# Sample-token attention in unsplit float32 on a tiled PE array

## The chip, the cores and the metric

The kernel runs on one core of a Trainium2 chip. The metric is the device time of one execution in microseconds (us). Three runs of the kernel before took 1849.01, 1849.45 and 1852.46 us; the median is 1849.45.

## The reference, cut to what matters

One decoder layer runs on a prompt of 1024 tokens and on 8 sequences of 4 new "sample" tokens each. The sample tokens attend to 1024 cached positions of their own sequence, which lie in pages of 128, and to the new tokens before them. This differential attention of the sample tokens is what the change touches: 4 heads, two score maps each (index m), and the second softmax is subtracted from the first with weight lambda.

```python
PAST_LEN, PAGE_SIZE, N_HEADS_A, HEAD_DIM_A = 1024, 128, 4, 64
...
def diff_attention(q, ks, vs, masks, lam):
    scale = HEAD_DIM_A ** -0.5
    s = jnp.concatenate([jnp.einsum('bqhmd,bkhmd->bhmqk', q, k, preferred_element_type=jnp.float32) * scale
                         for k in ks], -1)
    mask = jnp.concatenate(masks, -1)
    p = jax.nn.softmax(jnp.where(mask, s, -jnp.inf), axis=-1)
    a = (p[:, :, 0] - lam * p[:, :, 1]).astype(vs[0].dtype)
    offs = np.cumsum([0] + [k.shape[1] for k in ks]).tolist()
    return sum(jnp.einsum('bhqk,bkhe->bqhe', a[..., offs[i]:offs[i + 1]], vs[i]) for i in range(len(ks)))
```

The rest of the layer (projections, the HGRN2 branch, prompt attention, the gated merge, the convolutional FFN of width 2816) surrounds it and is unchanged.

## The kernel before, in words

The kernel writes each large float32 matrix product as three products of a high and a low half. `split` (lines 130 to 132) makes the halves: ScalarE (ACT) writes the high half in the format fp32r, VectorE (DVE) subtracts it from the source to get the low half. Such a product is then three TensorE (PE) matmuls, at lines 226 to 228 in `mm3` and 236 to 238 in `mm3s`. Small products are left in plain float32; the trace has two MATMUL records for each of those.

The order of the work: input projections, HGRN2, prompt attention, gates; then the merge of the first half of the prompt tokens; then `sample_attn`; then the FFN on the first half; then merge and FFN on the second half, with the sample tokens. The instructions of an engine are put in order when the program is built. `sample_attn` is written ahead of the FFN in the source, and the order that results has FFN matmuls (`mm<-hh,wh` and their like, 256 columns each) between those of the sample attention. At run time each engine goes through its list in that order; POOL's list also issues the gathers of cache pages.

`sample_attn` handles two groups (g) of four sequences (j). For the keys of a sequence it gathers two tiles of half the past (`pages`, line 715; 128 x 4 x 512 float32, 1 MB each; two buffers named `pg`). PE transposes each 128x128 piece (line 208, output `tp`, 32 a sequence), `split` turns PSUM into `kh` and `kl`, and two matmuls a head (lines 755 and 756, 64 columns of stationary queries, high beside low) give the scores in `ps_s`. ScalarE and VectorE fold them into `Pg`, whose 128 rows are 4 sequences x 32 (head, map, token). After the softmax, 8 small matmuls at line 792 turn `Pg` and subtract the second map, giving `aT`. For the values, VectorE and ScalarE split each gathered tile into `kh` and `kl`, and lines 816 and 817 multiply all four heads' rows by all four heads' values (512 columns); `hmask` keeps the diagonal blocks, and `select` (line 728) adds them up through a constant matrix. Line 801 does the same for the new tokens' values, and `sample_new_scores` (line 700), called before the last prompt head, made their scores.

Of the kernel before, what the change touches and what calls it, by code (L numbers as in the profile page):

```python
# [17 lines left out]
TP = 1024  # L18
TS = 32
# [12 lines left out]
C_SEL, C_SEL2, C_HM, C_M0, C_M1, C_CN, C_KEEP = 0, 128, 320, 324, 325, 326, 390  # L32
C_CAUS, C_ROPE, C_BD, C_IO, C_END = 390, 518, 1094, 1102, 1103
# [12 lines left out]
def hybrid_step(ctx: ExitStack, tc: tile.TileContext, I, O):  # L46
# [44 lines left out]
    sel2 = ck[:, C_SEL2:C_SEL2 + 192].rearrange("p (g c) -> p g c", c=32)  # L91
# [596 lines left out]

    def sample_new_scores():
        qbd_t = ring.get()  # L690
        qbd = qbd_t[:, :1024].rearrange("p (h b r) -> p h b r", b=8, h=4)
        V.memset(qbd_t[:, :1024], 0.0)
        for hh in range(4):
            for m in range(2):
                V.tensor_copy(qbd[m * 64:m * 64 + 64, hh, :, hh * 8 + m * 4:hh * 8 + m * 4 + 4],
                              qsm[m * 64:m * 64 + 64, hh].rearrange("p (b s) -> p b s", b=8))
# [5 lines left out]
        ring.put(qbd_t)  # L702

    def sample_attn(ap):
        def bank(tag):
            return ps_s.tile([128, 512], F32, tag="s", name="ps_s") if tag in ("sc", "av") else pst()

# [3 lines left out]
        def pages(nm, b, c):  # L711

            dst = ap.tile([128, 4, 512], F32, tag="pg", name="pg", bufs=2)
            i = b * 2 + c
            G.indirect_dma_start(dst.rearrange("p r e -> p (r e)"), None, crow[nm], bass.IndirectOffsetOnAxis(ap=idx[:, i:i + 1], axis=0))
            return dst

        def pair(tag):
            return ap.tile([128, 4, 256], F32R, tag=tag, name=tag, bufs=2)

        zero = ap.tile([128, 1], F32, name="zero")
        V.memset(zero, 0.0)
        osb = ap.tile([TS, 512], F32, name="osb")
        first = [True]

        def select(mk, sel):
            p = bank("ms")
            PE.matmul(p[:TS, :], lhsT=sel, rhs=mk, start=True, stop=True)
            if first[0]:
                evac("v", osb, p[:TS, :])  # L730
                first[0] = False
            else:
                V.tensor_tensor(osb, osb, p[:TS, :], ALU.add)

        def hmask(dst, src, np_):
            V.tensor_tensor(dst.rearrange("p (h e) -> p h e", h=4), src.rearrange("p (h e) -> p h e", h=4),
                            ck[:np_, C_HM:C_HM + 4][:, :, None].to_broadcast([np_, 4, 128]), ALU.mult)

        for g in range(2):
            qs = ap.tile([128, 4, 4, 2, 32], F32R, tag="qs", name="qs")  # L740
            V.tensor_copy(qs.rearrange("p b h x r -> p (b h x r)"), zero.to_broadcast([128, 1024]))
            for hh in range(4):
                for m in range(2):
                    r = slice(m * 64, m * 64 + 64)
                    c0 = hh * 8 + m * 4
                    src = qsm[r, hh, g * 16:g * 16 + 16].rearrange("p (b s) -> p b s", b=4)
# [4 lines left out]
            def scores(j, pr, ps, kth, ktl):  # L751
                for hh in range(4):
                    lq = qs[:, j, hh].rearrange("p x r -> p (x r)")
                    o = ps[:64, (pr % 2) * 256:(pr % 2 + 1) * 256]
                    PE.matmul(o, lhsT=lq, rhs=kth[:, hh], start=(hh == 0), stop=False)
                    PE.matmul(o, lhsT=lq, rhs=ktl[:, hh], start=False, stop=(hh == 3))
                if pr % 2:
                    pj = Pg[j * 32:j * 32 + 32, (pr // 2) * 512:(pr // 2) * 512 + 512]
                    evac("s", pj, ps[:32, :])
                    V.tensor_tensor(pj, pj, ps[32:64, :], ALU.add)  # L760

            late = None
            for j in range(4):
                b = g * 4 + j
                for pr in range(4):
                    if pr % 2 == 0:
                        ps = bank("sc")
                        kp = pages("cache_k", b, pr // 2)
                    kth, ktl = pair("kh"), pair("kl")
                    for c2 in range(2):  # L770
                        p = bank("kt").rearrange("p (h t) -> p h t", h=4)
                        for hh in range(4):
                            transpose(p[:, hh], kp[:, (pr % 2) * 2 + c2, hh * 128:(hh + 1) * 128])
                        split(p, kth[:, :, c2 * 128:c2 * 128 + 128], ktl[:, :, c2 * 128:c2 * 128 + 128])
                    if late:
                        scores(*late)
                    late = (j, pr, ps, kth, ktl)
            scores(*late)
# [6 lines left out]
            Cg = ap.tile([128, 128], F32, tag="Cg", name="Cg", bufs=2)  # L785
            V.tensor_scalar(Cg, selC, mx[:, 7:8], None, ALU.mult)
            aT = ap.tile([128, 8, 4, 2, 32], F32R, tag="aT", name="aT")
            for hf in range(2):
                p = bank("ms")
# [3 lines left out]
                pv = p.rearrange("p (c j r) -> p c j r", c=4, j=4)  # L793
                for c4 in range(4):
                    split(pv[:, c4], aT[:, hf * 4 + c4, :, 0], aT[:, hf * 4 + c4, :, 1])
            p = bank("ms")
# [3 lines left out]
            p = bank("ms")  # L800
            PE.matmul(p, lhsT=an, rhs=vs_, start=True, stop=True)
            mk = ap.tile([128, 512], F32, tag="mk", name="mk")
            hmask(mk, p, 128)
            select(mk, sel2[:, g])
            mk = None
            for j in range(4):
                b = g * 4 + j
                pav = bank("av")
                for c in range(8):
                    if c % 4 == 0:  # L810
                        vp = pages("cache_v", b, c // 4)
                    if c % 2 == 0:
                        vh, vl = (x.rearrange("p a b -> p (a b)").rearrange("p (r e) -> p r e", r=2) for x in (pair("kh"), pair("kl")))
                        split(vp[:, c % 4:c % 4 + 2], vh, vl)
                    la = aT[:, c, j].rearrange("p x r -> p (x r)")
                    PE.matmul(pav[:64], lhsT=la, rhs=vh[:, c % 2], start=(c == 0), stop=False)  # L816
                    PE.matmul(pav[:64], lhsT=la, rhs=vl[:, c % 2], start=False, stop=(c == 7))
                if j % 2 == 0:
                    mk = ap.tile([128, 512], F32, tag="mk", name="mk")
                r0 = (j % 2) * 64  # L820
                hmask(mk[r0:r0 + 64], pav[:64], 64)
                if j % 2:
                    select(mk, sel2[:, 2 + g * 2 + j // 2])
        ssq = ap.tile([TS, 4], F32, name="sssq")
        rs = ap.tile([TS, 4], F32, name="srs")
        sq = ap.tile([TS, 128], F32, name="ssq_")
        for hh in range(4):
            S.activation(sq, osb[:, hh * 128:(hh + 1) * 128], AF.Square, accum_out=ssq[:, hh:hh + 1])
        V.tensor_scalar(ssq, ssq, 1.0 / 128, EPS, ALU.mult, ALU.add)
        rstd(rs, ssq)  # L830
        p = bank("ms").rearrange("p (h t) -> p h t", h=4)
        for hh in range(4):
            V.tensor_scalar(osb[:, hh * 128:(hh + 1) * 128], osb[:, hh * 128:(hh + 1) * 128], rs[:, hh:hh + 1], None, ALU.mult)
            transpose(p[:, hh, :TS], osb[:, hh * 128:(hh + 1) * 128])
        oc = ap.tile([128, 4, TS], F32, name="soc")
        V.tensor_scalar(oc, p[:, :, :TS], SUBG, None, ALU.mult)
        G.dma_start(osc[4:8, :, TP:T].rearrange("h p t -> p h t"), oc)
# [350 lines left out]
def _consts():  # L1188
# [12 lines left out]
    j, q = r // 32, r % 32  # L1201
    h, m, s = q // 8, (q // 4) % 2, q % 4
# [82 lines left out]
```

## Time and profile before

| what | value |
|---|---|
| median of three runs | 1849.45 us |
| the profiled execution | 1850.71 us |
| its span, first to last instruction | 1848.5 us |
| PE busy | 1812.3 us, 98% of the span |
| DVE, ACT, POOL busy | 60%, 45%, 10% |
| mean granted TensorE clock | 0.994 of full speed |
| stretch with the sample attention | about 842 to 1151 us |

A busy PE in these views means that some matmul is under way. Matmuls overlap in the array, so a matmul's own duration (some 280 ns for 256 columns) is much longer than the time from its start to the next one's start (some 118 ns). What a matmul costs is read from starts, or from the chain of waits, which counts each stretch of time once.

### The profile page before, as it was taken

Reading aid. Unit: us, or ns where it says so; the run is one execution under the profiler, and the core shown is the slowest. Engines: PE = TensorE matmul, PEld = TensorE weight load, DVE = VectorE, ACT = ScalarE, POOL = GpSimd, SP = SyncE. Lnnn points to the kernel's source line nnn. Section 1 sums busy time; section 2 is a strip of 40 time slices with the busy share of each in tenths; the row PEclk is TensorE's granted clock in tenths of the full one; section 3 lists DMA queues with packets and bytes.
Section 4 is the critical chain, followed back from the end, with each engine's and each line's share of the span. In section 5 each row is a group of like instructions: output and inputs, shape, how many; then the busy total and the mean of one; then the engine's idle time right before and its main releaser. Section 6 shows DMA issues by size and latency. Waiting matters only on the chain.

```text
span 1848.5 us, 32245 instructions
## 1 busy us (share of the span) xinstructions
PE 1812.3 (98%) x12758; PEld 1700.8 (92%) x12758; DVE 1101.5 (60%) x2322; ACT 826.2 (45%) x1914; POOL 186.9 (10%) x245
## 2 busy tenths in 40 slices
PE   8999999999999999999999999999899999999996
PEld 8999999999999999879989987888887999999996
DVE  5757656754647554657776675543766655554336
ACT  6466253444554544346565564322425443343223
POOL 0000010120211010001111110000400000000103
PEclk9999999999999999999999999999999999999998
DMA  6110211221222115725555553433653332332334
GB/s 208 39 59 25 81 60 45 86 73 54 86 65 65 59 59 163 233 69 184 192 175 179 161 169 122 124 89 92 197 179 91 92 92 81 92 92 75 90 92 124
DMA packets 234794, 199.37 MB, mean 108 GB/s; under 512 B 8034, under 2 KB 213090, under 8 KB 230530
## 3 DMA queue, kind: packets, MB, share of 16 engines
q1 hardware_dynamic: 218432, 141.02, 25.4%
q0 software_dynamic: 9264, 47.44, 7.2%
q10 hardware_dynamic: 6948, 8.86, 1.4%
q8 instruction: 100, 1.64, 0.4%
q14 instruction: 50, 0.41, 0.1%
HBM read 173.10 MB, written 24.19 MB: 107 GB/s over the span
## 4 chain that ended last, share of the span: by engine, by line
PE 91%; DVE 4%; DMA 2%; ACT 1%; issue 1%; POOL 0%; SPq 0%; POOLq 0%; DVEq 0%; ACTq 0%
PE mm L237 14%; PE mm L238 14%; PE mm L236 14%; PE mm L226 10%; PE mm L228 10%; PE mm L227 10%; PE tp L208 4%; PE tp L663 2%; PE sb L406 2%; PE mm L247 1%; PE scp L636 1%; DMA c<-gsc 1%; PE scp L635 1%; PE mx L226 1%; PE ps_s L816 1%
## 5 line engine op out<-in xcount | busy, mean ns | idle before, releaser
L132 DVE TENSOR_TENSOR wl<-raw,wh 128x512 fp32r<-128x512 f32 (+1 forms) x404 | 287.7, 716 | 333.2 <-ACT wh L131 313.0
L131 ACT CAST wh<-raw 128x512 fp32r<-128x512 f32 (+1 forms) x404 | 244.9, 611 | 435.5 <-PE mm L237 335.1
L236 PE MATMUL mm<-hh,wh 128*128 128x256 f32 (+2 forms) x1312 | 384.9, 294 | 3.4 <-ACT hh L131 3.3
L237 PE MATMUL mm<-hl,wh 128*128 128x256 f32 (+2 forms) x1312 | 385.9, 294 | 1.6 <-DVE hl L132 0.9
L238 PE MATMUL mm<-hh,wl 128*128 128x256 f32 (+2 forms) x1312 | 386.0, 295 | 0.0
L236 PEld LDWEIGHTS mm<-hh,wh 128*128 128x128 f32 x1312 | 246.8, 188 | 13.4 <-ACT hh L131 4.0
L237 PEld LDWEIGHTS mm<-hl,wh 128*128 128x128 f32 x1312 | 246.8, 188 | 9.2 <-DVE hl L132 2.5
L238 PEld LDWEIGHTS mm<-hh,wl 128*128 128x128 f32 x1312 | 246.4, 188 | 5.8
L226 PE MATMUL mm<-xh,wh 128*128 128x384 f32 (+1 forms) x560 | 186.8, 334 | 0.6 <-ACT wh L131 0.5
L227 PE MATMUL mm<-xl,wh 128*128 128x384 f32 (+1 forms) x560 | 186.8, 334 | 0.0
L228 PE MATMUL mm<-xh,wl 128*128 128x384 f32 (+1 forms) x560 | 186.0, 332 | 0.0
L226 PE MATMUL mm<-wh,xh 128*128 128x256 f32 x480 | 136.5, 285 | 0.8 <-DVE rb L579 0.8
L227 PE MATMUL mm<-wl,xh 128*128 128x256 f32 x480 | 136.3, 284 | 0.2 <-DVE wl L132 0.2
L228 PE MATMUL mm<-wh,xl 128*128 128x256 f32 x480 | 135.9, 283 | 0.0
L226 PEld LDWEIGHTS mm<-xh,wh 128*128 128x128 f32 x560 | 105.3, 188 | 4.0 <-issue 2.3
L228 PEld LDWEIGHTS mm<-xh,wl 128*128 128x128 f32 x560 | 105.4, 188 | 1.8 <-issue 1.5
L227 PEld LDWEIGHTS mm<-xl,wh 128*128 128x128 f32 x560 | 105.4, 188 | 1.2 <-issue 0.8
L226 PEld LDWEIGHTS mm<-wh,xh 128*128 128x128 f32 x480 | 90.2, 188 | 1.5 <-issue 1.0
L227 PEld LDWEIGHTS mm<-wl,xh 128*128 128x128 f32 x480 | 90.4, 188 | 0.5 <-DVE wl L132 0.4
L228 PEld LDWEIGHTS mm<-wh,xl 128*128 128x128 f32 x480 | 90.4, 188 | 0.1
L204 ACT COPY s<-tp 128x512 f32<-128x512 f32 (+3 forms) x96 | 39.5, 426 | 101.6 <-PE tp L208 43.3
L1098 POOL TENSOR_TENSOR c<-hh,hl 128x512 f32<-128x512 f32 (+2 forms) x24 | 22.8, 948 | 504.4 <-DVE u20l L132 278.8
(680 smaller groups left out, 4067.9 us busy)
## 6 DMA issues: line engine op xcount, KB each, us to landing
raw<-in_w_up_dram SPq DMA_DIRECT2D x88, 512.0 KB, 3.8
raw<-in_w_in_dram SPq DMA_DIRECT2D x44, 512.0 KB, 4.0
raw<-in_w_down_dram SPq DMA_DIRECT2D x36, 512.0 KB, 3.8
raw<-in_w_out_dram SPq DMA_DIRECT2D x16, 512.0 KB, 3.4
raw<-in_w_down_dram SPq DMA_DIRECT2D x18, 384.0 KB, 3.4
gsc<-gt ACTq DMA_DIRECT2D x32, 192.0 KB, 1.9
raw<-in_w_branch_b_dram SPq DMA_DIRECT2D x16, 256.0 KB, 4.3
raw<-in_w_branch_a_dram SPq DMA_DIRECT2D x16, 256.0 KB, 4.0
```

What stands on the lines that cost most here:

```text
L131: S.copy(h, src)
L132: eng.tensor_tensor(l, src, h.bitcast(F32), ALU.subtract)
L204: S.copy(out, in_)
L208: PE.transpose(out, in_, ident[:n, :n])
L226: PE.matmul(ps, lhsT=ah, rhs=bh, start=(i == 0), stop=False)
L227: PE.matmul(ps, lhsT=ah, rhs=bl, start=False, stop=False)
L228: PE.matmul(ps, lhsT=al, rhs=bh, start=False, stop=(i == n - 1))
L236: PE.matmul(ps, lhsT=ah, rhs=bh, start=(k == 0), stop=False)
L237: PE.matmul(ps, lhsT=ah, rhs=bl, start=False, stop=False)
L238: PE.matmul(ps, lhsT=al, rhs=bh, start=False, stop=(k == n - 1))
L406: PE.matmul(p[:, a * 64:a * 64 + 64], lhsT=W[:, a * 128:a * 128 + 128], rhs=rhs[:, a * nb:a * nb + nb], start=True, stop=True)
L663: PE.matmul(po[:, :128], lhsT=aT[:, j * 128:(j + 1) * 128], rhs=v_[:, j], start=(j == 0), stop=(j == i))
```

## The change: what it does

Nothing of the sample attention is split into halves any more. Keys, queries, weights of the softmax and values stay float32.

- Keys: VectorE turns them in blocks of 32x32 (`V.transpose`, shown as STREAM_TRANSPOSE, four a sequence), from the gathered halves `pg` (two buffers) into `kT` (the buffer `pw`, one of it). A block of 32 partitions of `kT` holds 32 of the 128 past positions' numbers a, for one quarter c of a head's 128 dimensions.
- Scores: for each quarter c, row group a and head, one matmul with 32 rows, 32 columns of queries and 256 positions. Row group a writes a PSUM bank of its own, and head hh writes partitions 32hh to 32hh+31. That is 64 matmuls a sequence. `q2` holds the queries four times, once a row group; POOL writes it.
- Rows of `Pg` are now head x 32 (sequence, map, token).
- Values: each head has its own 32 columns of weights and its own 128 columns of values, and writes its own 32 partitions: 32 matmuls of 128 columns a sequence, straight from the gathered tiles (two halves in `pg`, or one whole tile in `pw`, in turn).
- The matmuls of `select` and `hmask` go; four vector operations with a column mask (C_JM) take the diagonal blocks.
- The norm and the write of the result are done for each group, not once.
- `sample_new_scores` makes its 8 products with 32 columns each.

```diff
     def sample_new_scores():
-        qbd_t = ring.get()
+        qn_t = ring.get()
...
         for g in range(2):
             for hh in range(4):
-                PE.matmul(pn[:, g], lhsT=qbd_t[:, (hh * 8 + g * 4) * 32:(hh * 8 + g * 4 + 4) * 32], rhs=ksm[:, hh], start=(hh == 0), stop=(hh == 3))
+                o = (g * 4 + hh) * 32
+                PE.matmul(pn[hh * 32:hh * 32 + 32, g], lhsT=qn_t[:, o:o + 32], rhs=ksm[:, hh], start=True, stop=True)
...
     def sample_attn(ap):
...
+        def half():
+            return ap.tile([128, 4, 512], F32, tag="pg", name="pg", bufs=2)
+
+        def whole():
+            return ap.tile([128, 8, 512], F32, tag="pw", name="pw")
...
+        q2 = ap.tile([128, 4, 4, 160], F32, name="q2")
+        G.memset(q2, 0.0)
+        qw = q2.rearrange("p c h (j x) -> p c h j x", x=40)
         for g in range(2):
...
-                    split(src, qs[r, :, hh, 0, c0:c0 + 4], qs[r, :, hh, 1, c0:c0 + 4])
+            for c in range(4):
+                src = qsm[c * 32:c * 32 + 32, :, g * 16:g * 16 + 16].rearrange("p h (j s) -> p h j s", j=4)
+                for a in range(4):
+                    G.tensor_copy(qw[a * 32:a * 32 + 32, c, :, :, (c // 2) * 4:(c // 2) * 4 + 4], src)
+            sc = [ps_s.tile([128, 512], F32, tag="s", name="ps_s")[:, :256] for _ in range(2)] + [pst()[:, :256] for _ in range(2)]
+            for j in range(4):
+                kT = whole().rearrange("p x y -> p (x y)").rearrange("p (k q t) -> p k q t", k=16, t=32)
+                for f in range(2):
+                    kp = half()
+                    pages(kp, "cache_k", g * 4 + j, f)
+                    for r in range(0, 4, 2):
+                        V.transpose(kT[:, :, f * 4 + r:f * 4 + r + 2].rearrange("p k q t -> p q k t"),
+                                    kp[:, r:r + 2].rearrange("p q (k t) -> p q k t", t=32))
+                for c in range(4):
+                    for a in range(4):
+                        ra = slice(a * 32, a * 32 + 32)
+                        for hh in range(4):
+                            PE.matmul(sc[a][hh * 32:hh * 32 + 32], lhsT=q2[ra, c, hh, j * 32:j * 32 + 32],
+                                      rhs=kT[ra, hh * 4 + c].rearrange("p q t -> p (q t)"),
+                                      start=(j + c == 0), stop=(j + c == 6))
...
-                        for hh in range(4):
-                            transpose(p[:, hh], kp[:, (pr % 2) * 2 + c2, hh * 128:(hh + 1) * 128])
-                        split(p, kth[:, :, c2 * 128:c2 * 128 + 128], ktl[:, :, c2 * 128:c2 * 128 + 128])
...
+            Pv = Pg[:, :TP].rearrange("p (q a t) -> p q a t", q=8, a=4)
+            for a in range(4):
+                evac("sv"[a % 2], Pv[:, :, a], sc[a].rearrange("p (q t) -> p q t", t=32))
...
+            po = pst()
+            pov = po.rearrange("p (j e) -> p j e", j=4)
+            for hh in range(4):
+                hr = slice(hh * 32, hh * 32 + 32)
+                PE.matmul(pov[hr], lhsT=an[:, hr], rhs=vs_[:, None, hh * 128:hh * 128 + 128].to_broadcast([TS, 4, 128]), start=True, stop=False)
             for j in range(4):
...
                 if j % 2:
-                    select(mk, sel2[:, 2 + g * 2 + j // 2])
+                    w = whole()
+                    vps = [w[:, :4], w[:, 4:]]
+                else:
+                    vps = [half(), half()]
+                for f in range(2):
+                    pages(vps[f], "cache_v", g * 4 + j, f)
+                for q in reversed(range(8)):
+                    for hh in range(4):
+                        hr = slice(hh * 32, hh * 32 + 32)
+                        PE.matmul(pov[hr, j], lhsT=aT[:, q, hr], rhs=vps[q // 4][:, q % 4, hh * 128:hh * 128 + 128],
+                                  start=False, stop=(j == 3 and q == 0))
+            osb = ap.tile([128, 128], F32, tag="osb", name="osb", bufs=2)
+            for j in range(4):
+                jm = ck[:, C_JM + j:C_JM + j + 1]
+                if j == 0:
+                    V.tensor_scalar(osb, pov[:, j], jm, None, ALU.mult)
+                else:
+                    V.scalar_tensor_tensor(osb, pov[:, j], jm, osb, ALU.mult, ALU.add)
...
```

The order on PE, in the key rounds of the first group. Before, transposes (`tp<-ident,pg`) and score matmuls (`ps_s<-kl,qs`) stand in small pieces between FFN matmuls:

```order
L208 MATMUL tp_9154<-ident_62,pg_9150 128x128 x4
L238 MATMUL mm_10574<-hh_8275,wl_10557 128x256
L208 MATMUL tp_9161<-ident_62,pg_9150 128x128 x4
L756 MATMUL ps_s_9106<-kl_9126,qs_9086 64x256
L755 MATMUL ps_s_9106<-kh_9125,qs_9086 64x256
```

Now the 64 matmuls of a sequence stand together: 16 such rows of four heads, of which the first five and the first FFN rows behind them are shown (`tp` and `ps_s` are the four row groups' banks, `pw` the turned keys).

```order
L744 MATMUL ps_s_9097<-pw_9174,q2_9079 32x256 x4
L744 MATMUL ps_s_9098<-pw_9174,q2_9079 32x256 x4
L744 MATMUL tp_9099<-pw_9174,q2_9079 32x256 x4
L744 MATMUL tp_9100<-pw_9174,q2_9079 32x256 x4
L744 MATMUL ps_s_9097<-pw_9174,q2_9079 32x256 x4
...
L236 MATMUL mm_10317<-hl_8272,wh_10250 128x256
```

Behind each such block of 64 come 38 to 46 FFN matmuls, then the next sequence's block, which reads the next `pw`.

The order on DVE around the turned keys of the second group (`wl` is the low half of an FFN weight, `c` the FFN's convolution):

```order
L738 STREAM_TRANSPOSE pw_9679<-pg_9680 128x2x16x32 x2
L738 STREAM_TRANSPOSE pw_9679<-pg_9684 128x2x16x32 x2
L131 TENSOR_TENSOR wl_10931<-raw_10924,wh_10930 128x512
L1051 TENSOR_TENSOR c_10799<-c_10799,mm_10860 128x256
L1051 TENSOR_TENSOR c_10799<-c_10799,mm_10861 128x256
L131 TENSOR_TENSOR wl_11053<-raw_11050,wh_11052 128x512
L131 TENSOR_TENSOR u5l_10859<-c_10799,u5h_10858 128x512
L738 STREAM_TRANSPOSE pw_9752<-pg_9753 128x2x16x32 x2
L738 STREAM_TRANSPOSE pw_9752<-pg_9757 128x2x16x32 x2
```

The four transposes of a sequence stand in a row, ahead of FFN work that was written later.

The order on POOL at the change from keys to values of the first group. Before, gather follows gather:

```order
L715 DMA pg_9468<-in_cache_k_dram,idx_72 128x2048
L715 DMA pg_9577<-in_cache_v_dram,idx_72 128x2048
L715 DMA pg_9595<-in_cache_v_dram,idx_72 128x2048
L715 DMA pg_9616<-in_cache_v_dram,idx_72 128x2048
L715 DMA pg_9634<-in_cache_v_dram,idx_72 128x2048
```

Now 15 of the 16 copies that write the second group's queries into `q2` stand between the gathers into `pg` and those into `pw`:

```order
L713 DMA pg_9429<-in_cache_v_dram,idx_72 128x2048
L713 DMA pg_9430<-in_cache_v_dram,idx_72 128x2048
L730 COPY q2_9079<-qsm_69 32x16x4 x15
L713 DMA pw_9465<-in_cache_v_dram,idx_72 128x2048 x2
L730 COPY q2_9079<-qsm_69 32x16x4
L713 DMA pg_9500<-in_cache_v_dram,idx_72 128x2048
L713 DMA pg_9501<-in_cache_v_dram,idx_72 128x2048
```

The copies overwrite what the first group's score matmuls read, so they stand behind these, and the gathers into `pw` behind the copies.

## Rows read from the trace of the kernel before

**Rows 1.** The page: busy time, share of the span, instructions of each engine.

```profile
PE 1812.3 (98%) x12758; PEld 1700.8 (92%) x12758; DVE 1101.5 (60%) x2322; ACT 826.2 (45%) x1914; POOL 186.9 (10%) x245
```

**Rows 2.** Busy time of each engine in a stretch, clock, DMA share and rate.

```profile
842.00:1151.00 309.00, 309.00 (x2297) 283.59 (x2296) 219.18 (x350) 172.71 (x334) 34.22 (x32) 1.00 0.52 170
```

**Rows 3.** The chain of waits in 842 to 1151 us, shares by line.

```profile
by line: PE mm L236 22.5%; PE mm L237 22.4%; PE mm L238 22.4%; PE tp L208 9.2%; PE ps_s L816 5.0%; PE ps_s L755 4.9%; PE ps_s L756 4.9%; PE ps_s L817 4.8%; PE tp L728 1.9%; PE tp L792 1.2%; PE tp L801 0.7%; PE tp L797 0.2%
```

**Rows 4.** PE in order of time: start, duration, what (line 792, plain float32).

```profile
930.41 0.28 PE L237 MATMUL mm<-hl,wh 128*128 128x256 f32 x1
930.53 0.28 PE L238 MATMUL mm<-hh,wl 128*128 128x256 f32 x1
930.64 1.95 PE L792 MATMUL tp<-Cg,Pg 128*128 128x128 f32 x16
932.35 0.36 PE L236 MATMUL mm<-hh,wh 128*128 128x256 f32 x1
```

**Rows 5.** PE in order of time: line 801 (32 rows), line 728 (32 columns).

```profile
941.74 1.12 PE L801 MATMUL tp<-vs__71,an 32*128 32x512 f32 x2
942.79 0.45 PE L817 MATMUL ps_s<-kl,aT 128*64 128x512 f32 x1
...
946.69 1.05 PE L728 MATMUL tp<-mk,ck 128*32 128x512 f32 x2
947.67 0.39 PE L236 MATMUL mm<-hh,wh 128*128 128x256 f32 x1
```

**Rows 6.** Stretches at line 399's pieces of 32 columns: PE and PEld records begun.

```profile
89.78:89.79 0.01, 0.01 (x2) 0.01 (x2) 1.00 0.00 0
89.78:89.83 0.06, 0.05 (x2) 0.05 (x4) 1.00 0.00 0
89.78:89.84 0.07, 0.07 (x4) 0.07 (x6) 1.00 0.00 0
89.78:89.88 0.10, 0.10 (x6) 0.10 (x8) 1.00 0.00 0
```

**Rows 7.** The same line's pieces of 64 columns.

```profile
303.77:303.87 0.10, 0.10 (x1) 0.10 (x2) 1.00 0.00 0
303.77:303.89 0.12, 0.12 (x2) 0.12 (x3) 1.00 0.00 0
303.77:303.94 0.17, 0.16 (x2) 0.16 (x3) 1.00 0.00 0
```

**Rows 8.** PE in order of time: line 700, the new tokens' scores.

```profile
665.16 1.87 PE L700 MATMUL tp<-ksm,s 128*128 128x32 f32 x16
666.87 0.63 PE L208 MATMUL tp<-ident,s 128*128 128x128 f32 x4
```

**Rows 9.** DVE by shape, 840 to 1145 us: busy us, mean ns, idle before.

```profile
L132 DVE TENSOR_TENSOR kl<-tp,kh 128x512 fp32r<-128x512 f32 x64 | 43.9, 689 | 18.9 <-ACT kh L131 18.0
L132 DVE TENSOR_TENSOR kl<-pg,kh 128x1024 fp32r<-128x1024 f32 x32 | 39.1, 1222 | 15.7 <-ACT kh L131 15.3
L741 DVE CAST qs<-zero 128x1024 fp32r<-128x1024 f32 x1 | 0.7, 693 | 1.0 <-PE ps_s L756 1.0
L780 DVE TENSOR_REDUCE mx<-Pg 128x1 f32<-128x1056 f32 x2 | 2.5, 1245 | 0.0
```

**Rows 10.** Line 715's gathers: ns min, median, max; first and last start.

```profile
L715 POOL DMA_INDIRECT pg<-in_cache_k_dram,idx x16: 935/1130/1402, 835.3 to 1040.1; - x16
DMA to landing us min/median/max: 5.5/6.0/8.0
```

**Rows 11.** DMA while the first two gathers run, 837.0 to 844.4 us.

```profile
DMA packets 541, 2.56 MB, mean 346 GB/s; under 512 B 50, under 2 KB 77, under 8 KB 285
q0 software_dynamic: 288, 2.10, 78.6%
```

**Rows 12.** POOL by shape, whole span: a copy near in size.

```profile
L628 POOL CAST qpad<-s 64x128 fp32r<-64x128 f32 x64 | 20.5, 320 | 176.1 <-PE scp L636 134.1 <-ACT s L595 19.9 <-PE scp L635 11.9
```

**Rows 13.** Stretches with a falling clock at the second merge (columns as rows 2).

```profile
1328.00:1333.00 5.00, 2.95 (x25) 2.75 (x24) 5.00 (x3) 0.62 (x1) 5.00 (x3) 1.00 0.36 105
1333.00:1340.00 7.00, 3.89 (x16) 3.90 (x17) 7.00 (x6) 0.00 (x0) 6.97 (x4) 0.51 0.28 78
```

More of the change, by code (lines that the diff above doesn't have):

```diff
@@ L689, in sample_new_scores @@
     def sample_new_scores():
[L690 to L693 removed]
+        qn_t = ring.get()
+        qn = qn_t[:, :256].rearrange("p (g h j r) -> p g h j r", g=2, h=4, j=4)
+        V.memset(qn_t[:, :256], 0.0)
+        for g in range(2):
             for m in range(2):
[L695 to L696 removed]
+                r = slice(m * 64, m * 64 + 64)
+                V.tensor_copy(qn[r, g, :, :, m * 4:m * 4 + 4],
+                              qsm[r, :, g * 16:g * 16 + 16].rearrange("p h (j s) -> p h j s", j=4))
         pn = pst()[:, :64].rearrange("p (g s) -> p g s", g=2)
@@ L699, in sample_new_scores @@
             for hh in range(4):
-                PE.matmul(pn[:, g], lhsT=qbd_t[:, (hh * 8 + g * 4) * 32:(hh * 8 + g * 4 + 4) * 32], rhs=ksm[:, hh], start=(hh == 0), stop=(hh == 3))
+                o = (g * 4 + hh) * 32
+                PE.matmul(pn[hh * 32:hh * 32 + 32, g], lhsT=qn_t[:, o:o + 32], rhs=ksm[:, hh], start=True, stop=True)
         V.tensor_tensor(sn, pn, ck[:, C_CN:C_CN + 64].rearrange("p (g s) -> p g s", g=2), ALU.add)
-        ring.put(qbd_t)
+        ring.put(qn_t)
     def sample_attn(ap):
-        def bank(tag):
-            return ps_s.tile([128, 512], F32, tag="s", name="ps_s") if tag in ("sc", "av") else pst()
@@ L718, in pair @@
[L718 to L733, printed above, removed]
@@ L748, in sample_attn @@
             Pg = ap.tile([128, T], F32, tag="Pg", name="Pg")
             S.copy(Pg[:, TP:T], sn[:, g])
[L751 to L760, printed above, removed]
@@ L792, in sample_attn @@
                     PE.matmul(p[:, c4 * 128:(c4 + 1) * 128], lhsT=Pg[:, c * 128:(c + 1) * 128], rhs=Cg, start=True, stop=True)
[L793 to L796, printed above, removed]
+                evac("s", aT[:, hf * 4:hf * 4 + 4], p.rearrange("p (c r) -> p c r", c=4))
+            p = pst()
             PE.matmul(p[:TS, :128], lhsT=Pg[:, TP:T], rhs=Cg, start=True, stop=True)
@@ L799, in sample_attn @@
             evac("v", an, p[:TS, :128])
[L800 to L805, printed above, removed]
-            for j in range(4):
[L807 to L821, printed above, removed]
-                if j % 2:
-                    select(mk, sel2[:, 2 + g * 2 + j // 2])
@@ L824, in sample_attn @@
[L824 to L834, printed above, removed]
@@ new lines, in sample_attn @@
+            V.tensor_scalar(mx[:, 4:5], mx[:, 4:5], 1.0 / 128, EPS, ALU.mult, ALU.add)
+            rstd(mx[:, 5:6], mx[:, 4:5])
+            V.tensor_scalar(osb, osb, mx[:, 5:6], None, ALU.mult)
+            p = pst()[:, :128]
+            transpose(p, osb)
+            oc = ap.tile([128, 4, 16], F32, tag="soc", name="soc")
+            V.tensor_scalar(oc, p.rearrange("p (h r) -> p h r", h=4)[:, :, :16], SUBG, None, ALU.mult)
+            G.dma_start(osc[4:8, :, TP + g * 16:TP + g * 16 + 16].rearrange("h p t -> p h t"), oc)
@@ L1200, in _consts @@
     c[:, C_ROPE:C_ROPE + 576] = rp.transpose(1, 0, 2, 3).reshape(128, 576)
-    j, q = r // 32, r % 32
-    h, m, s = q // 8, (q // 4) % 2, q % 4
-    c[r, C_SEL + j * 32 + h * 4 + s] = 1.0
-    sel2 = np.zeros((128, 8, 32), np.float32)
-    k = r[q < 16]
-    for g in range(2):
-        sel2[k, 2 + g, (g * 4 + k // 32) * 4 + k % 4] = 1.0
-        for jp in range(2):
-            sel2[k, 4 + g * 2 + jp, (g * 4 + jp * 2 + k // 64) * 4 + k % 4] = 1.0
-    c[:, C_SEL2:C_SEL2 + 192] = sel2[:, 2:].reshape(128, 192)
-    for hh in range(4):
-        c[:, C_HM + hh] = (q < 16) & (q // 4 == hh)
+    h, q = r // 32, r % 32
+    j, m, s = q // 8, (q // 4) % 2, q % 4
+    c[r, C_SEL + h * 32 + j * 4 + s] = 1.0
+    for jj in range(4):
+        c[:, C_JM + jj] = (q < 16) & (q // 4 == jj)
     c[:, C_M0] = m == 0
```

45 lines of the change are left out of this document (8 added, 37 removed).

## The prediction

> **What bounds the kernel now.** I read the page first: PE is busy for 98% of the span [rows 1], so what counts is the time that PE's list takes, and any wait that the change puts into it. Then the stretch in which the sample attention stands, 842 to 1151 us: PE is busy for all 309.0 us of it at the full clock, while DVE works 219 us, ACT 173 us, and the DMA engines are half used at 170 GB/s [rows 2]. So nothing but PE's own work sets the length of this stretch. Third, the chain of waits of the stretch, since it counts overlapping matmuls once [rows 3]: the FFN lines 236 to 238 hold 67.3% of it, 208 us; the rest is the sample attention, 101 us. Transposes (line 208) are 9.2%, scores (755, 756) 9.8%, values (816, 817) 9.8%, `select` (728) 1.9%, line 801 0.7%, lines 792 and 797 1.4%. Last I looked for what plain float32 and narrow pieces cost on PE, and for how fast a gather is.
>
> **What is removed.** All of this but lines 792 and 797, whose matmuls stay: 31.4% of 309 us = 97.0 us of PE time. Line 700 takes 1.71 us before the next instruction starts [rows 8]; its 8 products become narrow ones, some 0.3 us, so 1.4 us go there. The splits that go (44 and 39 us on DVE [rows 9], with their casts on ACT) lay beside PE and are worth nothing by themselves.
>
> **What is added on PE.** Line 792 does 8 plain float32 matmuls of 128 columns in 932.35 - 930.64 = 1.71 us, 0.214 us each, or 1.67 ns a column, in two passes [rows 4]. A piece with 32 rows or 32 columns alone isn't cheaper: 512 columns take 1.05 us and 0.98 us [rows 5], 0.855 us of columns and 0.13 to 0.2 us of filling and draining. So everything rests on how many narrow matmuls run side by side.
>
> The trace has one sight of it. Line 399 writes its 32-column pieces in turn to two different places of the array. Two records begin within 15 ns, four by 70 ns, six by 100 ns: two every 31 ns, each at about its own 32 columns' time [rows 6]. Its 64-column pieces all have one place, and there the second record begins only after the first is through, one at a time [rows 7]. So column groups do run side by side, both passes of them. No row shows four at once, nor row groups side by side. The bounds are then: scores, 512 matmuls of 256 columns at 0.427 us, 219 us one at a time and 13.7 us sixteen at a time; values, 256 of 128 columns, 54.8 us and 13.7 us. I take the lower ends, as the only row on tiles [rows 6] has no loss in it, with 0.01 us a round and some filling. Scores: 8 blocks x (4 rounds x 0.437 + 0.2) = 15.6 us. Values: 64 x 0.224 + 0.9 for six entries = 15.2 us. New tokens' values: 2 x 1.0 = 2.0 us. The two turns of the result: 0.2 us. In all 33.0 us. PE's work changes by -97.0 - 1.4 + 33.0 = **-65.4 us**.
>
> [...]
>
> **What waits are added.** PE's list is fixed. Between two blocks of 64 score matmuls it has mostly 40 FFN matmuls, at 0.118 us from start to start [rows 4] 4.7 us; with the block itself PE has 6.7 us of work in a key round. A round's data take longer. A `pg` buffer is refilled once its two transposes are done: 6.0 us from issue to landing [rows 10], then two transposes. A STREAM_TRANSPOSE isn't in this trace; operations on 1024 elements take from 693 to 1222 ns and a reduction 1245 [rows 9], I take 1.2 us. The lower end is 0.69; the upper I put at twice, 2.4. A round of a buffer is 6.0 + 2.4 + 0.3 for semaphores = 8.7 us (7.7 to 11.1), so PE waits 2.0 us, say 2.3 with other transfers in the way, in rounds 2 to 4 of both groups: 6 x 2.3 = 14 us (6 to 26). Behind a waiting score matmul stands the whole of the FFN; behind a waiting transpose on DVE stand low halves of later FFN weights, which PE doesn't reach before the block. The bandwidth alone would nearly do: two gathers take 78.6% of all engines for 7.4 us [rows 11], 2.9 us each at full use.
>
> At the end of the keys, the four moves out of PSUM, the maximum, the exponential with its table load and the factors take some 6.5 us one after another, against 4.7 us of FFN matmuls: 2 us. The gathers into `pw` stand on POOL behind 15 copies that wait for the last score matmul; at 320 ns or less [rows 12] these are 5 us, mostly covered by line 792 and what is around it. Behind the first value block four gathers follow each other, 16 us until the last has landed, against 14 us of PE work: 2 us, and 2 more where the pair before it lands late. So 6 us a group, 12 in all (2 to 20). Waits: 14 + 12 = **26 us** (8 to 46). The first blocks wait for nothing: in the order on PE 185 FFN matmuls, 22 us, stand ahead of them, enough for the memset, two gathers and four transposes.
>
> **Sum.** The profiled execution took 1850.71 us, its span 1848.5. 1850.7 - 65.4 + 26 = 1811.3; that execution lay 1.3 us above the median of the runs, so the forecast is **1810 us**. Its own range is 1790 to 1832, from the ends of the waits with a few us on the tiles.
>
> **The rivals.**
>
> *Two at a time (slower).* A float32 matmul has two passes on one tile. If the second pass of a matmul had to start before the next matmul's first, each would hold up the list for one pass, and only neighbours would overlap. Line 399's total time would be the same by this; its first two records would not begin together, and they do [rows 6], which speaks against it. Its price: scores 512 x 0.218 = 112 us, values 256 x 0.112 = 28.7, with the rest 144 us, so +45.6 us and hardly a wait: about 1897 us. The change is slower once a score matmul costs more than some 0.14 us. [...]
>
> *Row groups take turns.* Only the four heads overlap. A block is 16 x 0.437 + 0.2 = 7.2 us, 42 us more in all; a key round has then 11.9 us of PE work and waits for nothing. -65.4 + 42 + 12 = -11: 1838 us. For it: no row shows row groups; against it: each row group has its own bank.
>
> [...]
>
> *No waits.* The gathers land in time, or DVE is faster: 1784 us. For it: the DMA engines are half idle [rows 2]; against it: the 6 us of a landing were the rule over 32 gathers, not the exception [rows 10].
>
> **How the numbers follow.** My forecast 0.53, no waits 0.09, row groups in turn 0.11, the clock 0.08, two at a time 0.14, something else 0.05. A measurement of this kernel can tell 0.2%, 3.7 us, from no change. All but two at a time and some of the unknown are faster: 0.81; within 0.2%: 0.03; slower: 0.16. The range leaves out two at a time and little more: 1780 to 1858.
>
> **What would show it.** In the profile of the changed kernel: blocks of 64 score matmuls (128 records) of about 1.9 us, if row groups take turns 7 us, if two at a time 14 us; value blocks of 32 in 1.8 us; STREAM_TRANSPOSE of about 1.2 us; PE idle some 2 us ahead of each later score block, released by DVE's transposes and those by a DMA into `pg`; the sample attention over in some 145 us, not 309; a full clock there. I am wrong on PE if the blocks are long, and on the waits if PE is idle for under 8 or over 46 us in that stretch.

## The result, and the profile after

The changed kernel takes 1826.67 us, median of 4 runs (1823.2 to 1827.18), against 1850.42 (1849.01 to 1852.46): a ratio of 0.9867, 95% interval 0.985 to 0.9884. It is 24 us faster, where 40 were forecast (1810, range 1780 to 1858). The profiled execution took 1826.89 us, its span 1825.1.

Busy time of each engine on the page of the changed kernel, to be set beside [rows 1]:

```profile
PE 1769.4 (97%) x13652; PEld 1657.4 (91%) x13652; DVE 1036.4 (57%) x2199; ACT 747.7 (41%) x1774; POOL 200.7 (11%) x280
```

PE's busy time fell by 43 us, the span only by 23: there are waits now. The stretch of [rows 2], from 842 us to 1127, in three pieces (busy time of PE, PEld, DVE, ACT, POOL; clock; DMA share; GB/s):

```profile
842.00:851.00 9.00, 9.00 (x78) 8.99 (x76) 6.67 (x8) 3.27 (x8) 3.22 (x11) 1.00 0.74 256
851.00:1010.00 159.00, 138.00 (x2241) 118.49 (x2240) 86.16 (x135) 45.52 (x95) 38.92 (x50) 0.91 0.72 250
1010.00:1127.00 117.00, 117.00 (x851) 110.44 (x850) 63.59 (x103) 46.76 (x101) 1.89 (x2) 1.00 0.35 100
```

The last value block ends at 1007 us, 165 us into a stretch that took 309 (145 were forecast). In 851 to 1010 us PE is idle for 21 us and the clock is 0.91 on average; in the rows before and behind it PE is busy throughout at the full clock. What PE waited for in 842 to 1010 us (line, releaser: us in total, times, longest):

```profile
PE ps_s L744 <- DVE pw L738: 11.2, 4, 6.0
PE tp L789 <- DMA pw<-in_cache_v_dram,idx: 6.1, 1, 6.1
PE tp L207 <- DVE osb L802: 1.1, 1, 1.1
PE ps_s L766 <- ACT wh L130: 1.1, 1, 1.1
PE ps_s L766 <- DVE Cg L760: 1.0, 1, 1.0
```

Four stretches stand at half clock (0.50 granted), 27.3 us in all to their exact ends (columns as above; the last row is a score block at full clock):

```profile
863.40:870.20 6.80, 5.14 (x130) 3.49 (x131) 4.25 (x7) 1.55 (x3) 1.45 (x1) 0.50 0.85 274
904.40:911.10 6.70, 3.42 (x64) 2.96 (x64) 0.00 (x0) 0.00 (x0) 2.14 (x3) 0.50 0.51 175
938.50:948.70 10.20, 10.20 (x76) 6.07 (x69) 2.68 (x4) 0.64 (x2) 0.84 (x1) 0.50 0.19 53
972.60:976.00 3.40, 3.11 (x100) 2.20 (x102) 3.28 (x6) 0.05 (x1) 1.12 (x1) 0.50 0.42 77
874.84:877.52 2.68, 2.68 (x129) 1.81 (x128) 2.07 (x4) 1.13 (x2) 0.93 (x1) 1.00 0.92 348
```

The first two begin inside the two waits of 6 us, the last one inside a wait of 2.8 us, the third in a block that PE got in pieces. PE in order of time there (start, duration, what, count; in brackets the idle time before and what ended it):

```profile
934.72 1.96 PE L744 MATMUL ps_s<-pw,q 32*32 32x256 f32 x64
937.80 0.33 PE L207 MATMUL tp<-ident,osb 128*128 128x128 f32 x1 [1.12 <-DVE osb L802]
938.05 3.27 PE L744 MATMUL tp<-pw,q 32*32 32x256 f32 x32
...
942.41 3.64 PE L744 MATMUL tp<-pw,q 32*32 32x256 f32 x32
```

The second group's first score block comes as 64 records of two row groups, the turn of the first group's result, and two times 32 records of one row group alone. Its third and fourth row groups need the `tp` banks that the first group's result still holds.

And a whole block at full clock (two records a matmul):

```profile
874.84 0.45 PE L744 MATMUL ps_s<-pw,q 32*32 32x256 f32 x8
874.89 0.44 PE L744 MATMUL tp<-pw,q 32*32 32x256 f32 x8
875.08 0.42 PE L744 MATMUL ps_s<-pw,q 32*32 32x256 f32 x8
875.13 0.42 PE L744 MATMUL tp<-pw,q 32*32 32x256 f32 x8
875.30 0.69 PE L744 MATMUL ps_s<-pw,q 32*32 32x256 f32 x9
```

Each matmul has two records here, read as its two passes. The first passes of all sixteen tiles start within 0.1 us, their second passes from 0.24 us on; the seventeenth matmul starts at 0.46 us, after its tile's own 0.43. But the eighteenth starts 0.19 us after it. A round of sixteen so takes 0.647 us instead of 0.437, and the block 2.68. Two of the eight blocks go so; three others at full clock take 2.92 to 2.95 us, and what makes their last 0.25 us isn't shown.

POOL in the first key rounds:

```profile
836.43 1.08 POOL L713 DMA_INDIRECT pg<-in_cache_k_dram,idx  x1 [0.17 <-issue]
837.82 0.98 POOL L713 DMA_INDIRECT pg<-in_cache_k_dram,idx  x1 [0.30 <-issue]
838.80 1.58 POOL L730 COPY q<-qsm 32x64 f32<-32x64 f32 x4
847.20 4.46 POOL L730 COPY q<-qsm 32x64 f32<-32x64 f32 x12 [6.82 <-DMA pg<-in_cache_k_dram,idx]
851.93 1.12 POOL L713 DMA_INDIRECT pg<-in_cache_k_dram,idx  x1 [0.27 <-POOL q L730]
```

DVE has turned the first `pg` by 847 us:

```profile
844.57 2.37 DVE L738 STREAM_TRANSPOSE pw<-pg 128x1024 f32<-128x1024 f32 x2 [2.29 <-DMA pg<-in_cache_k_dram,idx]
```

Twelve of the copies into `q2` start only when the two gathers have landed, and the next gathers stand behind them, though `pg` was free at 847 us. In the second group's copies the same happens twice:

```profile
892.88 4.72 POOL L730 COPY q<-qsm 32x64 f32<-32x64 f32 x11 [5.21 <-DMA pg<-in_cache_v_dram,idx]
897.87 0.97 POOL L713 DMA_INDIRECT pw<-in_cache_v_dram,idx  x1 [0.27 <-POOL q L730]
907.76 0.23 POOL L730 COPY q<-qsm 32x64 f32<-32x64 f32 x1 [7.53 <-DMA pw<-in_cache_v_dram,idx]
```

The gathers of values behind the copies start at 897.87 and 908.50 us, the first of these 10 us after `pw` was free. The waits stand in the list of instructions itself, three on the copies' line, each ended by the landing of a gather (after 6.82, 5.21 and 7.53 us); so they come from how the program was built and not from GpSimd:

```profile
L730 POOLq EVENT_SEMAPHORE  x3: 17/17/43, 847.1 to 907.7; - x3
```

### The profile page after: what moved, and what is told of

Read it like the earlier page. It is cut to its first block, busy times and chain, and to the rows that moved or that the text cites. A ratio compares the mean times of both kernels' runs of the same rounds, so it can differ in the third digit from the quotient of the medians.

```text
span 1825.1 us, 33731 instructions
## 1 busy us (share of the span) xinstructions
PE 1769.4 (97%) x13652; PEld 1657.4 (91%) x13652; DVE 1036.4 (57%) x2199; ACT 747.7 (41%) x1774; POOL 200.7 (11%) x280
## 4 chain that ended last, share of the span: by engine, by line
PE 85%; DMA 5%; DVE 5%; issue 2%; ACT 1%; POOL 1%; SPq 0%; POOLq 0%; DVEq 0%; ACTq 0%
PE mm L237 13%; PE mm L236 12%; PE mm L235 12%; PE mm L225 11%; PE mm L227 10%; PE mm L226 10%; PE tp L207 3%; DMA pg<-in_cache_k_dram,idx 3%; PE tp L662 2%; PE sb L405 2%; PE mm L246 1%; PE scp L635 1%; PE scp L634 1%; DVE pw L738 1%; PE mx L225 1%
```

## The experiments

**Which part pays.** The kernel before with the new values alone:

```diff
+ half(), both(): four 8 KB tiles for the pages of values
+ Cg by head, new values into po, JM masks (as in the changed kernel)
  qs, transposes, splits, scores: as before
```

> The kernel before with the new way of the values alone (32-column pieces by head into one bank, JM masks) and the old keys: transposes, splits and 64-row scores as before. Four 8 KB tiles hold the pages of values. By the sums of the two traces: values, their splits, the selecting products and the four turns took 30.1 + 5.9 + 2.1 = 38.1 us of PE, the new ones 16.7 + 2.0 us with 3.6 us of it from half clock: -19 to -23 us on PE, and at most 5 us of waits: 1831 us (1827 to 1836) against 1850.4. The keys would then be worth only 4 us net of the 23.7 us in all. Rival (the values cause the waits, the keys pay): 1838 to 1850, with PE waiting for gathers of values by more than 8 us.

Measured: 1830.53 us (1829.98 to 1832.78), ratio 0.9899 (0.9883 to 0.9914), within the range that was expected. PE hardly waits and has its full clock:

```profile
842.00:1010.00 168.00, 167.63 (x1613) 164.65 (x1612) 108.78 (x189) 88.64 (x184) 23.76 (x23) 1.00 0.59 200
```

So 19 of the 24 us are the values', and the keys, which should have brought the most (55 us of transposes and scores removed), bring 4 net on top of them; the new keys alone were not run. The rest of the study is on the keys' waits.

**The copies.** On ACT instead of POOL:

```diff
-                    G.tensor_copy(qw[a * 32:...
+                    S.copy(qw[a * 32:...
```

> The changed kernel with the 2 x 16 copies into q2 (L730) on ACT instead of POOL; nothing else. Theory C: the two waits of 6 us ahead of the second score block (865.06) and in the first group's values (907.68) come from POOL's copies, which stand ahead of the next gathers and wait for the landing of the two before. Then those gathers start some 5 to 10 us sooner, both waits shrink to 0 to 1.5 us (-10 us of idle), and the two stretches of 6.8 us at half clock behind them go too (-6.8 us): 1809 us (1805 to 1814), against 1826.7 of the changed kernel. Rival L: the waits are the loop of gather, landing and two transposes itself, whoever makes the copies: 1823 to 1828, the waits still 5 to 6 us. Rival A: sixteen copies on ACT behind the last score block of the first group hold up the moves out of PSUM that stand behind them: the wait ahead of the softmax turn (893 us) grows from 1 to 4 or 5 us, and the gain is 3 to 4 us less, about 1813.

Measured: 1820.21 us (1816.22 to 1823.16), 6 us less, not 17. PE's waits in 842 to 1010 us:

```profile
PE ps_s L744 <- DVE pw L738: 5.4, 3, 2.7
PE ps_s L766 <- ACT wh L130: 3.1, 1, 3.1
```

The wait for `pw` pages is gone (6.1 us), the one at the second score block is 2.7 instead of 6.0. Theory C holds on the one and on 3.3 us of the other; the 2.7 left are more than its 1.5 and fit the loop of rival L. Rival A comes true too: 3.1 us ahead of the softmax turn, where 1.1 were. But the half clock did not go with the waits: 20.5 us of it in this stretch in place of 27.3, all of it now while PE works (5.3 of the 27.3 us lay in waits), and 3.4 more at 828 us, ahead of the sample attention.

**Two q2 tiles**, so that the second group's copies wait for no block:

```diff
-        q2 = ap.tile([128, 4, 4, 160], F32, name="q2")
+        qq = [ap.tile([128, 4, 4, 104], F32, name=f"q2{g}") for g in range(2)]
...
-                    G.tensor_copy(qw[a * 32:a * 32 + 32, c, ...], src)
+                    S.copy(qw[:, :, :96]...[:, :, :, o:o + 4], src[:, :, :3])
+                    S.copy(qw[:, :, 96 + o:100 + o], src[:, :, 3])
```

The first copy takes three of a group's four sequences, the second the fourth.

> The changed kernel with one q2 tile for each group, packed closer (104 columns a head instead of 160), the first group's copies on ACT ahead of everything, the second group's on ACT behind the first score block; so no copy waits for the last score block of the first group. Copies are twice as many and half as large. Theory C: as with the copies on ACT alone, without their place ahead of the softmax: 1806 us (1802 to 1812). Rival L (the loop itself makes the waits): 1822 to 1828. If rival A is right and C too, this one is 3 to 4 us faster than the one with the copies on ACT in the old place; if A is wrong they are equal within 2 us.

Measured: 1822.32 us (1819.46 to 1825.82); missed. The wait ahead of the first group's softmax turn fell to 0.7 us, but PE waited 5.65 us at 843 us for an FFN move behind these copies on ACT: both groups' copies had been put ahead of everything. With one copy in place of the two halves:

> The kernel with two packed q2 tiles again, each filled by 16 copies on ACT in place of 32 halves. Theory: in the run with 32 halves PE waited 5.65 us at 843 us for an FFN move out of PSUM on ACT (L203), which stood behind the copies; with 16 copies that wait is gone, and half-clock stretches of 3.4 us around it: -6 to -8 us against 1822.3: 1815 us (1812 to 1819); so some 5 us faster than the copies on ACT in the old place (1820.2), whose wait ahead of the softmax was 3.1 us. Rival: the half-clock stretches move elsewhere and the time stays at 1819 to 1823.

Measured: 1814.77 us (1813.12 to 1816.24), as expected, though of the wait at 841 us 2.9 us are left. With two tiles PE's list changes too: the second group's first score block comes in two pieces here (56 and 72 records) and takes 7.4 us with its waits, in the changed kernel 11.3. So some 4 of the 12 us gained are that block's and not the copies'.

**The split block.** The first group's result turned after the second group's scores:

```diff
-            p = pst()[:, :128]
-            transpose(p, osb)
...
+            late = osb
...
+            if late is not None:
+                turned(0, late)
```

> The changed kernel, in which the first group's result is turned (and stored) only when the second group's scores have left PSUM; its copies stay on POOL. Then all 64 matmuls of the second group's first score block stand together on PE, where the changed kernel has 32, the turn, 16 and 16 of one row group each. Theory B: that split block (3.08 + 3.20 + 3.57 = 9.85 us, against 2.7 us for a whole one) and the 10.2 us at half clock from 938.5 on come from the bank that the result held: -7.1 us on the block, -1.1 us of wait for osb, -1.4 us on FFN matmuls at half clock: 1817 us (1814 to 1820), against 1826.7. Rival: the clock falls there anyway, or the whole block waits for the last bank as long as its parts did: 1823 to 1828.

Measured: 1814.58 us (1813.37 to 1818.92), ratio 0.981 (0.9797 to 0.9824): 12 us, where 9.7 were expected. PE's waits are nearly those of the changed kernel (18.5 us in 842 to 1010 us, 21.0 there), so most of the gain is the block and the clock. The stretch, and the same block:

```profile
851.00:1010.00 159.00, 140.47 (x2246) 126.00 (x2219) 91.48 (x144) 48.44 (x102) 38.31 (x49) 0.95 0.73 257
932.23:935.18 2.95, 2.95 (x129) 2.07 (x129) 2.49 (x7) 0.81 (x5) 1.07 (x1) 1.00 0.93 305
```

It is whole, takes 2.95 us to the next matmul, and no half clock follows it. 17.1 us of half clock remain, behind the two long waits and one of 2.5 us. The edit did one thing more: 49 or 50 FFN matmuls now stand between the second group's blocks, where 40 to 44 stood, which gives the pages more time; what that is worth was not isolated.

**Both edits** (two tiles, 16 copies each, late turn):

> Both edits together: two packed q2 tiles filled by 16 copies each on ACT, and the first group's result turned late. If both theories hold, their gains add: 1826.7 - 11 - 9 = 1807 us (1803 to 1812), with PE idle for 6 to 9 us in the stretch of the sample attention and 10 us or less at half clock. If the clock falls after whatever wait is left, 1812 to 1818.

Measured: 1812.02 us (1811.66 to 1812.32), ratio 0.9791 (0.9777 to 0.9804) to the kernel before: the fastest version, 15 us below the changed kernel and 18 below the values alone. The gains of 12 and 12 do not add: both shorten the split block, 13.3 us of idle are left in 842 to 1010 us, and of 17.1 us at half clock (3.4 of them at 826 us) a new stretch of 6.8 stands behind a wait of 3.3 us at 882 us.

```profile
842.00:1010.00 168.00, 154.73 (x2442) 139.47 (x2441) 103.34 (x158) 58.94 (x129) 32.74 (x34) 0.96 0.74 263
```

**The loop of a `pg` buffer.** One packed q2 tile, copies on ACT, late turn, with two buffers and with three:

```diff
-            return ap.tile([128, 4, 512], F32, tag="pg", name="pg", bufs=2)
+            return ap.tile([128, 4, 512], F32, tag="pg", name="pg", bufs=3)
```

> One q2 tile for both groups, packed (104 columns a head), its 2 x 16 copies on ACT, and the first group's result turned late; an, sq share Cg's memory and osb has one buffer, to make room for the next kernel, of which this is the twin. Two pg buffers as before. Sum: the copies on ACT alone took 1820.2 us, the late turn gave 12 us on the changed kernel, of which the wait for osb and the split block were there too in the run with the copies on ACT: 1820.2 - 8 = 1812 us (1808 to 1817), PE idle 10 to 13 us in the sample attention, the wait ahead of the first group's softmax turn still 3 us.

> The same with three pg buffers instead of two. Theory L: the waits of 1 to 3.5 us ahead of score blocks that are left come from the loop of a pg buffer (gather, landing, two transposes); with a third buffer the next pages are under way a half sooner, the waits fall from 5 or 6 us in all to under 2 us, and a half-clock stretch or two behind them go: -4 to -8 us against its twin, 1806 us (1802 to 1809). Rival V: the transposes wait in DVE's list (behind FFN splits, and until the block before has left pw): waits and time stay within 2 us of the twin, and the pages land before the transposes start.

Measured: 1814.85 us (1810.11 to 1815.79) with two, 1823.12 (1820.88 to 1825.99) with three. Theory L's time falls: the version with a third buffer is 8 us slower. Four of the six waits ahead of score blocks do go, but the two left are longer (5.5 and 3.5 us), and the half clock grows. Two buffers, then three:

```profile
842.00:1010.00 168.00, 155.99 (x2443) 138.04 (x2442) 101.64 (x158) 59.88 (x132) 33.52 (x34) 0.98 0.76 261
842.00:1010.00 168.00, 151.26 (x2356) 133.48 (x2355) 97.13 (x148) 55.69 (x125) 32.64 (x33) 0.92 0.71 254
```

PE is idle for 16.7 us in place of 12.0, and 27.3 us stand at half clock in place of 6.8. Of rival V the mechanism holds (the pages land before the transposes start), its time does not. ACT, then DVE, in the kernel with three:

```profile
858.35 1.14 ACT L130 CAST wh<-raw 128x512 fp32r<-128x512 f32 x2 [2.30 <-DMA raw<-in_w_up_dram]
```

```profile
859.00 0.69 DVE L131 TENSOR_TENSOR wl<-raw,wh 128x512 fp32r<-128x512 f32 x1 [2.23 <-ACT wh L130]
859.61 4.62 DVE L750 STREAM_TRANSPOSE pw<-pg 128x1024 f32<-128x1024 f32 x4
```

The second block's pages were asked for at 839.67 and 846.36 us and take some 8 us. The transposes stand behind the low half of an FFN weight, which waits for ACT, which waits for the weight's DMA; PE is idle for 5.5 us there, and for 3.5 us at 930 in the same way (ACT waits 6.2 us for a weight). Weight loads and key gathers in 835 to 980 us (count, KB each, median us to landing), of the kernel before:

```profile
raw<-in_w_up_dram SPq DMA_DIRECT2D x17, 512.0 KB, 3.8
pg<-in_cache_k_dram,idx POOLq DMA_INDIRECT x10, 6.2
```

of the changed one:

```profile
raw<-in_w_up_dram SPq DMA_DIRECT2D x14, 512.0 KB, 7.5
pg<-in_cache_k_dram,idx POOLq DMA_INDIRECT x16, 7.2
```

of the twin with two buffers:

```profile
raw<-in_w_up_dram SPq DMA_DIRECT2D x15, 512.0 KB, 6.3
pg<-in_cache_k_dram,idx POOLq DMA_INDIRECT x16, 7.4
```

and with three buffers:

```profile
raw<-in_w_up_dram SPq DMA_DIRECT2D x14, 512.0 KB, 8.1
pg<-in_cache_k_dram,idx POOLq DMA_INDIRECT x16, 7.8
```

The gathers are as many with two buffers as with three, but with three one more of them is under way at a time, and the weights land 1.8 us later. That the one slows the other was not isolated. A rival stands beside it: the edit also changed PE's list. Between the first value blocks and the second group's first score block stand 153 FFN matmuls with three buffers and 173 with two, at 0.118 us each 2.4 us less for that block's pages; there lie the wait of 3.5 us, one of 1.2 for a bank still held, and 10.2 us at half clock. The wait of 5.5 us has no such difference ahead of it.

**The tiles.** Row groups 0 and 1 first, then 2 and 3, so that eight tiles take turns:

```diff
-                for c in range(4):
-                    for a in range(4):
+                for ap2 in ((0, 1), (2, 3)):
+                    for c in range(4):
+                        for a in ap2:
```

> The changed kernel with the 64 score matmuls of a block in another order: row groups 0 and 1 for all four c, then 2 and 3, so that 8 tiles instead of 16 take turns. Theory Q: a matmul of 256 float32 columns holds its tile for some 0.43 us and few matmuls can be under way, so 8 at a time make a block 8 x 0.43 + 0.2 = 3.6 us (3.4 to 3.9) at full clock instead of 2.7, and +7 us in all, about 1833. Rival D: matmuls leave PE's queue at a fixed 41 ns each, whatever tile they go to: the block stays at 2.6 to 2.8 us, and the time within 3 us of 1826.7.

Measured: 1828.2 us (2 runs, 1826.57 and 1829.83). A block at full clock, and PE's wait in the key rounds:

```profile
863.09:866.77 3.68, 3.68 (x128) 2.75 (x128) 2.14 (x4) 1.14 (x2) 1.45 (x1) 1.00 0.81 276
PE ps_s L745 <- DVE pw L738: 3.3, 3, 2.0
```

3.5 to 3.7 us in five of the six blocks at full clock, as theory Q says: 8 rounds of 0.43 and filling (the first block took 5.8, 0.3 of it in stops without a releaser). A distance of 41 ns whatever the tile falls; as a lower bound it isn't excluded, since eight tiles alone give 54 ns. The time did not follow the block (0.8 us more in each of eight would be +6.4, measured +1.5), as PE waited 9 us less; that a longer block is time for the pages is the likely reason. The last run asks for that lower bound, with half as many columns in twice as many matmuls, on the kernel with the late turn:

```diff
-                for c in range(4):
+                for c, n in ((c, n) for c in range(4) for n in range(2)):
```

> The kernel with the late turn, each score matmul of 256 columns cut into two of 128: 128 matmuls a block, sixteen tiles in turn as before (the first halves of all sixteen, then the second). A block of 64 took 2.69 us at full clock, four rounds of 0.647 us, of which 0.43 us is a tile's own work; with 8 tiles in turn a block took 3.5 to 3.7 us. Theory Q (a round of sixteen loses 0.19 to 0.22 us because the next round can't be taken up before matmuls have drained): 8 rounds x (0.214 + 0.2) = 3.3 us (3.1 to 3.6). Rival D (no two matmuls less than 41 ns apart over a block, whatever their length): 128 x 41 ns = 5.2 us. Rival C (a limit on the columns that the array takes in a time): 2.6 to 2.8 us as before. The time follows the block: +5, +20 or 0 us against 1814.6.

Measured: 1853.21 us (1850.22 to 1854.74), far from all three. In one stretch in which the matmuls flow at full clock, 82 passes, or 41 matmuls, begin in 1.09 us (second count, PEld):

```profile
848.89:849.98 1.09, 1.09 (x94) 1.07 (x82) 1.09 (x3) 1.08 (x2) 0.76 (x3) 1.00 0.05 15
```

That is 26.6 ns a matmul and 0.425 us a round of sixteen, as theory Q has it (0.414); D's 41 ns and C's 0.32 us fall. By this stretch the loss of some 0.2 us a round has no part that grows with the columns. But whole blocks took 7.3 to 10.7 us, far from Q's 3.3, and 44 us stand at half clock (mean clock 0.87 in 842 to 1010 us). The time went into something none of the theories had:

```profile
PE tp L753 <- issue: 22.0, 12, 5.7
PE ps_s L753 <- issue: 4.9, 3, 4.3
```

PE stands still for up to 5.7 us in the middle of blocks and waits for nothing that the engines' rows show. The DMA rows show something: a queue of kind `instruction`, of 16 KB a transfer, in the changed kernel and in this one:

```profile
q8 instruction: 107, 1.75, 0.4%
q8 instruction: 115, 1.88, 0.4%
```

Eight transfers more go with 1024 matmul records and 1024 weight loads more. Seven of the stops last over 1.5 us, and each ends 1.3 to 1.5 us after such a transfer has ended; the one from 891.34 to 895.66 us has its transfer from 893.37 to 894.36. So the long stops go with these transfers; that PE waited there for its own instructions, 512 a block here, is my reading of the queue's kind, and no edit tested it.

## Why the prediction was right, and what was off

The direction and the range were right, the time was 17 us low. By PE's list from the first FFN matmul to the first turn of `c`, the FFN's convolution (each record's time until the next one starts, gaps over 0.05 us counted as idle), 376.1 us before and 354.7 after; line 700 lies ahead of it:

| step | predicted | measured |
|---|---|---|
| removed (lines 208, 755, 756, 816, 817, 728, 801, turns) | -97.0 | -93.9 |
| line 700 | -1.4 | -1.6 |
| scores | +15.6 | +31.5 |
| values | +15.2 | +16.7 |
| new tokens' values, turns | +2.2 | +2.3 |
| waits | +26 | +20.4 |
| FFN matmuls and lines 766, 769 longer | 0 | +1.6 |

The measured steps make -23.0 us, the two profiled executions differ by 23.8.

**The scores are the term that failed.** "4 rounds x 0.437 + 0.2" has no loss in a round; the measured round is 0.647 us, the block 2.7 us at best, 21.6 us for eight. The trace of line 399 [rows 6] had only two places of the array in turn, six records begun in 0.10 us, so it could not show the loss. Sixteen tiles do 16 x 0.427 / 0.647 = 10.6 times the work of one here, and 16 x 0.214 / 0.425 = 8.1 times at 128 columns (estimates from the measured rounds and the 0.214 us of [rows 4]), where the prediction took sixteen times. The remaining 9.9 us: 6.0 are the split block (8.7 instead of 2.7 us, about half of it from half clock), 3.2 two blocks that ran at half clock wholly or in part (4.6 us at 865, 4.0 at 973), 0.7 the three blocks of 2.9.

**The rivals.** Two at a time is out: sixteen first passes begin within 0.1 us, ahead of the first matmul's second pass at 0.24 us. Row groups do not take turns: a block has 2.7 us, not 7.2. The clock, given 0.08, came true in part: 27.3 us at half clock (the kernel before has such a stretch in [rows 13]), some 10 us of loss (4 on FFN and values, 6 on scores; an estimate, half of PE's busy time there). The full clock that was forecast for the sample attention was gone inside the two waits of 6 us and one of 2.8 us; at the waits of 1.0 to 1.3 us it mostly held.

**The waits** had the right size and partly the wrong cause. In the key rounds 11.2 us against 14, but 6.0 of them in one round, of which 3.3 went with POOL's copies; of the others three are 1.2, 1.3 and 2.8 us and two are none, where 2.3 were put on each. In softmax and values 9.3 us against 12, and 6.1 of it again the copies. I had counted their 5 us on POOL and the wait for the last score block, not that they wait for the landing of gathers issued ahead of them, and so hold the next ones. The 0.3 us put on semaphores in that sum was read from no row; in the changed kernel the next gather into a `pg` starts 0.3 us after that buffer's second transpose has ended (861.75 after 861.47 us). The bank of the first group's result was not in the working at all; the late turn, which frees it, was worth 12 us. That the sum of the waits came out near is in part luck.

**Held:** the transposes on DVE (1.2 us, measured 1203 ns), a value block (1.8 us, measured 1.88), the new tokens' values (1.0 a group), and "the first blocks wait for nothing".

## What to carry to other kernels

When work leaves a PE-bound stretch, look at what stands in line on the engines that now have to deliver: here moving the copies that stood on GpSimd ahead of gathers was worth 6 us (12 with a second tile and another order on PE), freeing a PSUM bank held by an unrelated result 12, and both together 15, where the whole change had brought 24. Price small tiles by a round that was measured with as many tiles under way, and keep their work in one piece: a quarter of a block, alone on its four tiles, took 1.86 us at full clock (in the run with the copies on ACT), the whole block 2.7 to 2.95.

```profile
931.85:933.71 1.86, 1.86 (x34) 0.90 (x33) 0.54 (x2) 0.71 (x2) 0.84 (x1) 1.00 1.00 304
```

Before giving a freed buffer to a transfer, see whether that transfer is late, and read the new order of the lists: with a third buffer for gathers the weights landed later and the kernel was slower.

## What the runs showed of the hardware

- Sixteen 32x32 float32 tiles: a round takes a tile's own time and some 0.2 us more, for 256 columns (0.647 us) and, in one stretch, for 128 (0.425 us); with eight tiles the loss isn't seen (3.5 to 3.7 us for 8 rounds of 0.43). Blocks wholly at half clock took 4.45 to 4.8 us in four of the kernels (4.58 in the changed one, from 865.06 us on), 1.7 to 1.8 times the best and not twice. That would fit a loss that doesn't follow the clock (4 x (0.86 + 0.2) + 0.1 = 4.3, an estimate from the 0.43 us of a tile and the loss at full clock), but isn't shown by it.
- On sixteen tiles the two records of a float32 matmul are not kept together: the first records of fifteen other tiles start between them (from 874.84 on, the second ones from 875.08 us on).
- With twice as many matmuls of half the columns PE stood for 27 us in all without a releaser on any engine; the stops over 1.5 us end 1.3 to 1.5 us after a 16 KB transfer of kind `instruction`.
- In all versions with 16 gathers of keys in 835 to 980 us (10 before) a 512 KB weight load landed in 6.3 to 8.2 us (a run's median) instead of 3.8; the 1 MB gathers of keys took 5.8 to 7.8 instead of 6.2, so not always longer.
